# A two-layer hybrid trunk on one core: four small changes, and three branch outputs transposed by a detour through DRAM

## The chip, the cores and the metric

The kernel runs on one core of one Trainium2 chip. The metric is the device time of one execution in microseconds. A profile is one more execution, recorded by the hardware; its span is counted from the first to the last instruction of the core, and its own time lies a little above the span.

## The reference

Two layers with 256 tokens and a width of 2048. Cut to what matters:

```
for l in range(2):
    xn = rmsnorm(h, pre_norm_g[l])
    fq fk fv ff fg dq dk dv dg sz sxbc sdt su sg mg = columns of xn @ w_in[l]
    oa = forgetting_attention(fq, fk, fv, ff + b) * silu(fg)      # bias: cumsum(log_sigmoid(ff)), 4 heads
    ob = differential_attention(rope(dq), rope(dk), dv) * silu(dg)
    oc = mamba2_ssd(sz, sxbc, sdt)
    od = s5(su) * silu(sg)                                       # diagonal complex scan, gelu, GLU
    m  = sum_n sigmoid(mg[n]) * (o_n @ w_branch[l, n])           # each o_n has 512 columns, m has 2048
    h  = h + rmsnorm(m @ w_out[l], post_norm_g[l])
```

Inputs and output are float32.

## The kernel before, in words

**Tiles and staging.** Tokens lie in two blocks of 128 (`tb`). All weights of both layers are streamed once, as 298 chunks of 512 rows by 512 columns (524 for one segment), each four k-tiles of 128 rows. SyncE's queue loads a chunk into `raw` (1 MB, three buffers). float32 products are made from two rounded halves: ScalarE writes `wh`, the rounded weights, VectorE `wl`, the rest (`raw` − `wh`), both for two k-tiles at once (128x1024); the pools of `wh` and of `wl` hold five such pairs each. The input of a matmul is split in the same way into `xh` and `xl` (for a branch output `oh` and `ol`, for the merged sum `mh` and `ml`). For each k-tile and token block TensorE then does three matmuls of 128x512, `wh·xh` (L425), `wh·xl` (L426) and `wl·xh` (L427), into the accumulator `acc`. L115 is the helper `act` of ScalarE, L103, L109 and L112 are helpers of VectorE.

**Order.** `plan()` gives the column groups of a layer: first the thirteen input segments (fq fk fv bc fg dq dk dv dg xs sz su sg), then for the branches n = 0, 1, 2 (fox, diff, ssd) four pairs of a gate group `mg(n, cg)` of 16 k-tiles and a projection `br(n, cg)` of four, then the fourth branch (S5) with its GLU, then `out`, four groups. `group()` goes over the chunks of one group; a `hook` runs a function at one chunk of it.

**The branches.** Each is a generator, resumed between two chunks (`pump`) for a budget of work; `yield WAIT` makes it stop until the next chunk, and `drain` runs it to its end. The framework's scheduler then orders the instructions of each engine. In the fox generator, twelve float32 matmuls of 128x128 with broadcast operands (L480, L483) make the running sums of the log forget gates for the mask tiles `bm`. In S5, `prep_b` transposes `u`, splits it into `uu` and sends it to DRAM (`du`) and back (`s5u`); the drive matmul (L887) reads `s5u`, and a scan on VectorE (L905) follows.

**Branch outputs.** The output of a branch (`fxo`, `dfo`, `xst` for n = 0, 1, 2) has tokens on the partitions, and as input of `br(n, ...)` it must have channels there. `o_split`, hooked at chunk 2 of `mg(n, 0)`, does this with eight PE transposes (L300, by `split_T`), and ScalarE and VectorE split the result from PSUM into `oh` and `ol`. Elsewhere the kernel already transposes by a detour: `put` (L320) writes a tile to DRAM as four blocks of 32 columns by token, `get` (L326) reads it back as `shuf` with the blocks spread over partitions, both on GpSimd's queue, and VectorE's 32x32 transpose does the rest (`xT`, `foxqT`, `mT` and others).

**The ends.** At the start SyncE's queue brings the first columns of x and the first chunk in pieces; the gain `g0` comes on ScalarE's queue. At the end, for each token block, the square sum of the last output group is added up, a root is taken on VectorE, `y` is multiplied with the gain `pg` and added to `h` in four pieces of 512 columns, and SyncE sends each (L1210).

Of the kernel before, what the change touches and what calls it, by code (L numbers as in the profile page):

```python
# [23 lines left out]
PAD = 112  # L24
# [5 lines left out]
WAIT = -1  # L30
# [41 lines left out]
def trunk(ctx: ExitStack, tc: tile.TileContext, x, xT0, wall, cst, prm, rows, lam, normg, postg, s5b, s5c, out):  # L72
# [65 lines left out]
    g0 = cp.tile([128, KT], F32, name="g0")  # L138
    side = A.dma_start(out=g0, in_=prm[0, :, P_PRE:P_PRE + KT]).ins
    with tc.issue_after(side):  # L140
        act(warm, warm, AF.Exp)
    x0 = [wlp.tile([128, 4, 256], F32, tag="wl", name="x0") for _ in range(2)]
    load(x0[0], xT0[:, 0:4])
# [3 lines left out]
    strict_r = cp.tile([128, 128], F32R, name="strict_r")  # L147
    mask2 = cs[:, C_MK:C_MK + 256]
# [174 lines left out]
    def get(d):  # L323

        X = blk("shuf", (128, 4, 128))
        nc.gpsimd.dma_start(out=X, in_=d.rearrange("j (t i) c -> (j t) i c", i=4))  # L326
        return X
# [14 lines left out]
    def prefetch(spread=False, also=None):  # L342
# [6 lines left out]
        for k0, k1 in zip(cuts, cuts[1:]):  # L349
            load(raw[:, k0:k1], src[:, k0:k1])  # L350
# [113 lines left out]
    def fox(st):  # L464
# [316 lines left out]
    def s5(st):  # L781
# [55 lines left out]
        def prep_a(pc):  # L837
# [11 lines left out]
            uu, d = blk("uu", (128, 2, 256), F32R), dp.tile([128, 2, 256], F32R, tag="du", name="du")  # L849
            act(uu[:, 0], psu[:, 0:256])  # L850
            tt(uu[:, 1], psu[:, 0:256], uu[:, 0].bitcast(F32), SUB)
            ud[pc] = blk("ud", (128, 256))
            act(ud[pc], psu[:, 0:256], AF.Copy, scale=pk[:, l, P_D + pc:P_D + pc + 1])
# [82 lines left out]
        yield WAIT  # L936
        yield table(0)
# [28 lines left out]
    for l in range(L):  # L966
# [3 lines left out]
        if l == 0:  # L970
# [25 lines left out]
            def x_first(k):  # L996
                split_x(k, x0[k // 4][:, k % 4])

            prefetch(spread=True, also=x_first)
            load(x0[1], xT0[:, 4:8])  # L1000

# [12 lines left out]
            def more(c):  # L1014
# [6 lines left out]
                elif c == 7:  # L1021
                    prefetch()
                    load(cs, cst)
                    act(strict_r, strict)
                    load(pk, prm.rearrange("l p n -> p l n"))
# [43 lines left out]
        zz = small([128, 2, 12], "zz")  # L1069
# [32 lines left out]

        def turn_m(q):
            for tb in range(2):
                split_T(lambda i: mstat(tb, 4 * q, 4), m[tb][q], 4, scale=0.5)
        for gi, (kind, arg, ncol, nk) in enumerate(plan()):
            if kind == "in":
# [11 lines left out]
                group(xstat, nk, ncol, ev)  # L1119
                have.add(arg)  # L1120
            elif kind == "mg":
# [10 lines left out]
                def turn_o(n=n):  # L1132
                    if n < 3:
                        drain(("fox", "diff", "ssd")[n])
                    o_split(st, n)
                hook = {2: turn_o} if cg == (2 if n == 3 else 0) else None
# [52 lines left out]
            else:  # L1189
                cg = arg  # L1190
                if cg == 0:
                    yss = small([128, 2, 4], "yss")
# [135 lines left out]
```

## Time and profile before

| | |
|---|---|
| time, median of 3 runs | 1759.68 us (1759.61 to 1761.12) |
| time of the profiled execution | 1759.27 us |
| its span | 1757.4 us |
| TensorE busy | 1736.9 us (99%) |
| VectorE busy | 1340.6 us (76%) |
| ScalarE busy | 840.9 us (48%) |
| GpSimd busy | 87.4 us (5%) |
[...]
| moved by DMA | 356.51 MB, 203 GB/s in the mean |

Busy time is the time in which an engine has an instruction in work; waiting, and the issue of transfers, are not counted. TensorE's chain of waits, and not the shares of the others, says what an edit elsewhere is worth.

### The profile page before, as it was taken

How to read it: one execution, taken by the hardware profiler on the slowest of the kernel's cores; microseconds unless marked ns; L12 is line 12 of the kernel's file. 1: busy time of each engine (PE TensorE's matmuls, PEld its weight loads, DVE VectorE, ACT ScalarE, POOL GpSimd, SP SyncE). 2: the span in 40 equal slices, each digit the busy share in tenths (PEclk: the TensorE clock that was granted, in tenths of full speed). 3: DMA queues.
4: the chain of work that ended last, by engine and by line, in shares of the span. 5: the costliest groups of instructions: out<-in, count | busy, mean ns of one | idle time of the engine just before them, and what ended most of it. 6: DMA issues, size and time to landing. Idle time of an engine off the chain costs nothing.

```text
span 1757.4 us, 22117 instructions
## 1 busy us (share of the span) xinstructions
PE 1736.9 (99%) x8150; PEld 1438.2 (82%) x8150; DVE 1340.6 (76%) x2415; ACT 840.9 (48%) x1135; POOL 87.4 (5%) x146
## 2 busy tenths in 40 slices
PE   9999999999999999999999999999999999999997
PEld 7888888888888878888889888888888888788886
DVE  6765467997899999576674655669978999985854
ACT  7445445554444434444464444564544444444542
POOL 0000020000100000020000000100010000000100
PEclk9999999999999999999999999999999999999999
DMA  9664574455655655585555645744555655555752
GB/s 359 229 223 157 193 276 168 145 215 181 194 218 186 222 185 199 189 290 188 181 195 206 227 145 197 269 168 164 198 191 195 221 172 197 214 191 192 275 204 96
DMA packets 60813, 356.51 MB, mean 203 GB/s; under 512 B 7840, under 2 KB 12064, under 8 KB 22304
## 3 DMA queue, kind: packets, MB, share of 16 engines
q1 hardware_dynamic: 46640, 322.04, 51.2%
q0 software_dynamic: 13920, 33.04, 5.9%
q8 instruction: 64, 1.05, 0.2%
q14 instruction: 45, 0.37, 0.1%
q10 hardware_dynamic: 144, 0.01, 0.0%
HBM read 341.43 MB, written 13.63 MB: 202 GB/s over the span
## 4 chain that ended last, share of the span: by engine, by line
PE 85%; DVE 10%; issue 2%; DMA 2%; ACT 1%; SPq 0%; POOL 0%; DVEq 0%; ACTq 0%
PE acc L427 27%; PE acc L425 27%; PE acc L426 27%; DVE wl L103 3%; DVE Et L103 1%; DVE s5w L103 1%; DVE s5t L103 1%; PE mx L300 1%; DVE s5a L103 1%; DVE s5a L905 1%; PE mx L595 1%; DVE Etm L103 1%; PE mx L462 1%; DVE m L103 1%; DMA s5u<-du 1%
## 5 line engine op out<-in xcount | busy, mean ns | idle before, releaser
L115 ACT ACTIVATE wh<-raw 128x1024 fp32r<-128x1024 f32 (+1 forms) x586 | 619.0, 1061 | 730.9 <-PE acc L426 616.0
L103 DVE TENSOR_TENSOR wl<-raw,wh 128x1024 fp32r<-128x1024 f32 (+1 forms) x586 | 712.0, 1221 | 324.0 <-ACT wh L115 311.6
L425 PE MATMUL acc<-wh,xh 128*128 128x512 f32 (+1 forms) x1896 | 730.8, 386 | 1.2 <-ACT sig L115 1.2
L427 PE MATMUL acc<-wl,xh 128*128 128x512 f32 (+1 forms) x1896 | 725.6, 384 | 3.4 <-DVE wl L103 3.3
L426 PE MATMUL acc<-wh,xl 128*128 128x512 f32 (+1 forms) x1896 | 726.1, 383 | 0.0
L427 PEld LDWEIGHTS acc<-wl,xh 128*128 128x128 f32 x1896 | 355.4, 188 | 74.9 <-DVE wl L103 6.3
L425 PEld LDWEIGHTS acc<-wh,xh 128*128 128x128 f32 x1896 | 356.2, 188 | 71.6 <-ACT sig L115 2.1
L426 PEld LDWEIGHTS acc<-wh,xl 128*128 128x128 f32 x1896 | 356.3, 188 | 66.9
L425 PE MATMUL acc<-wh,oh 128*128 128x512 f32 x256 | 100.5, 393 | 0.0
L426 PE MATMUL acc<-wh,ol 128*128 128x512 f32 x256 | 99.8, 390 | 0.0
L427 PE MATMUL acc<-wl,oh 128*128 128x512 f32 x256 | 99.7, 389 | 0.0
L425 PE MATMUL acc<-wh,mh 128*128 128x512 f32 x224 | 87.5, 391 | 0.0
L427 PE MATMUL acc<-wl,mh 128*128 128x512 f32 x224 | 87.3, 390 | 0.0
L426 PE MATMUL acc<-wh,ml 128*128 128x512 f32 x224 | 87.2, 389 | 0.0
L115 ACT ACTIVATE sig<-acc,rhalf 128x512 f32<-128x512 f32 x64 | 42.7, 683 | 32.6 <-PE acc L427 24.9
L425 PEld LDWEIGHTS acc<-wh,oh 128*128 128x128 f32 x256 | 48.1, 188 | 10.5 <-issue 0.8
L427 PEld LDWEIGHTS acc<-wl,oh 128*128 128x128 f32 x256 | 48.1, 188 | 10.2
L426 PEld LDWEIGHTS acc<-wh,ol 128*128 128x128 f32 x256 | 48.1, 188 | 9.5
L427 PEld LDWEIGHTS acc<-wl,mh 128*128 128x128 f32 x224 | 42.1, 188 | 8.7
L426 PEld LDWEIGHTS acc<-wh,ml 128*128 128x128 f32 x224 | 42.1, 188 | 8.6
L425 PEld LDWEIGHTS acc<-wh,mh 128*128 128x128 f32 x224 | 42.1, 188 | 8.5
L905 DVE TENSOR_TENSOR_SCAN s5a<-S5R,s5w 128x256 f32<-128x256 f32 x64 | 40.4, 672 | 0.0
(339 smaller groups left out, 1376.6 us busy)
## 6 DMA issues: line engine op xcount, KB each, us to landing
raw<-in_wall_dram SPq DMA_DIRECT2D x290, 1024.0 KB, 4.8
shuf<-d POOLq DMA_DIRECT2D x36, 256.0 KB, 5.6
raw<-in_wall_dram SPq DMA_DIRECT2D x8, 1048.0 KB, 5.1
s5b<-in_s5b_dram POOLq DMA_DIRECT2D x16, 256.0 KB, 3.3
s5u<-du POOLq DMA_DIRECT2D x32, 128.0 KB, 3.6
d<-m POOLq DMA_DIRECT2D x12, 256.0 KB, 4.6
h<-in_x_dram SPq DMA_DIRECT2D x2, 1024.0 KB, 9.7
d<-ropea POOLq DMA_DIRECT2D x8, 256.0 KB, 2.8
```

The costliest lines, as they stand in the source:

```text
L103: V.tensor_tensor(out=out, in0=a, in1=b, op=op)
L115: A.activation(out, a, f, **kw)
L300: PE.transpose(ps[:, i * 128:(i + 1) * 128], src[:, i * 128:(i + 1) * 128], ident)
L425: PE.matmul(o, lhsT=sh, rhs=rh, start=k == 0, stop=False)
L426: PE.matmul(o, lhsT=sl, rhs=rh, start=False, stop=False)
L427: PE.matmul(o, lhsT=sh, rhs=rl, start=False, stop=k == nk - 1)
L462: PE.matmul(pso[:, c], lhsT=pt[:, b], rhs=v[b][:, c], start=b == 0, stop=b == nb - 1)
L595: PE.matmul(ps[:, a, 0:nk], lhsT=qT[hd // 2][a][:, hd % 2, qb * 128:(qb + 1) * 128], rhs=kT[hd // 2][:, hd % 2, 0:nk], start=True, stop=True)
L905: V.tensor_tensor_scan(out=a[:, r], data0=rr, data1=w[:, r], initial=0.0, op0=MUL, op1=ADD)
```

## The change

Five parts:

1. **Start.** The gain and the first k-tile of x are one tile `gx`, loaded by one transfer on ScalarE's queue; k-tile 1 and k-tiles 2 and 3 are loaded on SyncE's queue in turn with the pieces of the first chunk, and k-tiles 4 to 7 behind it.
2. **Bias.** Each of two key blocks is made by two matmuls of 128x512 in the rounded format (a product `fU` of the upper triangle and the gates, from VectorE, high and low half, against a column of ones). The second block takes its carry from the last column of `bm[hd][:, 1]`. The generator yields 2.2 and not 0.8.
3. **S5.** `ud` is made ahead of `uu`'s low half, and one more `yield WAIT` stands behind `prep_b(0)`.
4. **End.** In the last layer `y` is multiplied with the gain first, three of the four square sums are added ahead, `h` is updated in five pieces (512, 512, 512, 256, 256), and for the second token block every second piece is sent on ScalarE's queue.
5. **Branch outputs.** For n = 0, 1, 2 the eight PE transposes become `put` and `get` on ScalarE's queue, two of each per branch and layer, and one VectorE transpose of 128x512 per token block. The writes stand at chunk 0 of `sg`, of `mg(0, 3)` and of `mg(1, 3)`, each behind a `drain`; the reads at chunk 0 of `mg(n, 0)`; the transposes at chunk 2 of it, as before. The rows of `w_br` are permuted to fit.

```diff
-    def put(src):
+    def put(src, eng=nc.gpsimd):
         d = dp.tile([4, 128, 128], F32, tag="d", name="d")
-        nc.gpsimd.dma_start(out=d.rearrange("j n c -> n j c"), in_=src.rearrange("n (j c) -> n j c", j=4))
+        eng.dma_start(out=d.rearrange("j n c -> n j c"), in_=src.rearrange("n (j c) -> n j c", j=4))
...
         bm = [blk("bm", (128, 3, 128)) for _ in range(4)]
+        fh, fl = small([128, 2, 4], "fh", F32R, 1), small([128, 2, 4], "fl", F32R, 1)
+        V.tensor_copy(fh, lf[:, :, 0:4])
+        tt(fl, lf[:, :, 0:4], fh.bitcast(F32), SUB)
         for kb in range(2):
             ps = mx()
+            for j, a in enumerate((fh, fl)):
+                o = blk("fU", dt=F32R)
+                tt(o.rearrange("p (h t) -> p h t", h=4), U.unsqueeze(1).to_broadcast([128, 4, 128]),
+                   bc(a.bitcast(F32)[:, kb].unsqueeze(2), [128, 4, 128]), MUL)
+                PE.matmul(ps, lhsT=bc(one_r, [128, 128]), rhs=o, start=j == 0, stop=j == 1)
+            p3 = ps.rearrange("p (h k) -> p h k", h=4)
             for hd in range(4):
-                o = ps[:, hd * 128:(hd + 1) * 128]
-                PE.matmul(o, lhsT=bc(lf[:, 0, hd:hd + 1], [128, 128]), rhs=bc(one, [128, 128]) if kb else U,
-                          start=True, stop=kb == 0)
-                if kb:
-                    PE.matmul(o, lhsT=bc(lf[:, 1, hd:hd + 1], [128, 128]), rhs=U, start=False, stop=True)
-            p3 = ps.rearrange("p (h k) -> p h k", h=4)
-            for hd in range(4):
-                tt(bm[hd][:, 2 * kb], p3[:, hd], tri, ADD)
                 if kb == 0:
+                    tt(bm[hd][:, 0], p3[:, hd], tri, ADD)
                     act(bm[hd][:, 1], p3[:, hd])
-            yield 0.8
+                else:
+                    stt(bm[hd][:, 2], p3[:, hd], bm[hd][:, 1, 127:128], tri, ADD, ADD)
+            yield 2.2
...
+    def o_put(st, n):
+        for tb in range(2):
+            st["o", n, tb] = put(st["o", n, tb], A)
+
+    def o_get(st, n):
+        for tb in range(2):
+            st["o", n, tb] = get(st["o", n, tb], A)
     def o_split(st, n):
...
-            split_T(lambda i: (oh, ol), st["o", n, tb], 4)
+            if n == 3:
+                split_T(lambda i: (oh, ol), st["o", n, tb], 4)
+            else:
+                r = blk("oT", (128, 4, 128))
+                V.transpose(out=r.rearrange("p k (t i) -> p i k t", i=4),
+                            in_=st["o", n, tb].rearrange("p i (k c) -> p i k c", c=32))
+                act(oh, r)
+                tt(ol, r, oh.bitcast(F32), SUB)
...
         yield prep_b(0)
         yield WAIT
+        yield WAIT
         yield table(0)
...
+        def send_o(n):
+            drain(("fox", "diff", "ssd")[n])
+            o_put(st, n)
...
-                group(xstat, nk, ncol, ev)
+                group(xstat, nk, ncol, ev, hook={0: lambda: send_o(0)} if arg == "sg" else None)
...
-                hook = {2: turn_o} if cg == (2 if n == 3 else 0) else None
+                hook = {2: turn_o} if cg == (2 if n == 3 else 0) else {}
+                if n < 3 and cg == 0:
+                    hook[0] = lambda n=n: o_get(st, n)
+                if n < 2 and cg == 3:
+                    hook[0] = lambda n=n: send_o(n + 1)
...
+                    if l == L - 1:
+                        tt(yb[tb][3], last, pg[3], MUL)
+                        tt(s1, ysum[:, tb], yss[:, tb, 3:4], ADD)
+                        rsqrt(r1, s1, 1, 1.0 / D, EPS)
+                        rows = slice(tb * 128, (tb + 1) * 128)
+                        for i, (c0, c1) in enumerate(((0, 512), (512, 1024), (1024, 1536), (1536, 1792), (1792, 2048))):
+                            y = yb[tb][c0 // 512][:, c0 % 512:c0 % 512 + c1 - c0]
+                            stt(h[tb][:, c0:c1], y, r1, h[tb][:, c0:c1], MUL, ADD)
+                            (A if tb and i % 2 else nc.sync).dma_start(out=out[rows, c0:c1], in_=h[tb][:, c0:c1])
+                        return
```

TensorE, in the input segments of the first layer, where the mask tiles are made. Of before, the last matmul ahead of the bias and the bias (L480 and L483 are its two calls):

```order
L427 MATMUL acc<-wl,xh 128x512
L480 MATMUL mx<-cs,sp 128x128 x5
L483 MATMUL mx<-cs,sp 128x128
L480 MATMUL mx<-cs,sp 128x128
L483 MATMUL mx<-cs,sp 128x128
L480 MATMUL mx<-cs,sp 128x128
L483 MATMUL mx<-cs,sp 128x128
L480 MATMUL mx<-cs,sp 128x128
L483 MATMUL mx<-cs,sp 128x128
L425 MATMUL acc<-wh,xh 128x512
```

And of the change, the first of the two places, whose matmuls with weights have the lines L429 to L431 there; the second place comes a chunk later and has the same rows:

```order
L431 MATMUL acc<-wl,xh 128x512
L490 MATMUL mx<-fU,one_r 128x512 x2
L429 MATMUL acc<-wh,xh 128x512
L430 MATMUL acc<-wh,xl 128x512
L431 MATMUL acc<-wl,xh 128x512
```

Twelve matmuls in one place became two pairs in two places.

ScalarE, around the end of the diff branch in the first layer (`dfo` are its two outputs, `pt` its scores, `oh` the fox output). Before:

```order
L115 ACTIVATE pt<-mx 128x256
L115 ACTIVATE wh<-raw 128x1024 x2
L115 ACTIVATE pt<-mx 128x256
L115 ACTIVATE dfo<-mx 128x512
L115 ACTIVATE wh<-raw 128x1024 x4
L115 ACTIVATE oh<-mx 128x512 x2
L115 ACTIVATE wh<-raw 128x1024
```

And in the change, where L328 is a read and L322 a write on ScalarE's queue:

```order
L115 ACTIVATE pt<-mx 128x256
L328 DMA shuf<-d 128x512 x2
L115 ACTIVATE wh<-raw 128x1024 x2
L115 ACTIVATE pt<-mx 128x256
L115 ACTIVATE dfo<-mx 128x512
L322 DMA d<-dfo 128x4x128
L115 ACTIVATE wh<-raw 128x1024 x2
L115 ACTIVATE oh<-oT 128x512
L115 ACTIVATE wh<-raw 128x1024
L322 DMA d<-dfo 128x4x128
L115 ACTIVATE oh<-oT 128x512
```

The two writes of `dfo` stand between the splits of weights, the first right behind the copy of `dfo`'s second block; three `wh` and one `oh` stand between them.

VectorE, where the third branch's output is turned in the first layer. Before, `ol` is made from PSUM:

```order
L103 TENSOR_TENSOR wl<-raw,wh 128x1024
L103 TENSOR_TENSOR s5t<-s5a,Et 128x512
L103 TENSOR_TENSOR s5w<-s5a,Et 128x512
L103 TENSOR_TENSOR wl<-raw,wh 128x1024
L103 TENSOR_TENSOR ol<-mx,oh 128x512 x2
L103 TENSOR_TENSOR s5a<-s5w,s5t 128x256 x2
```

And in the change:

```order
L103 TENSOR_TENSOR wl<-raw,wh 128x1024
L103 TENSOR_TENSOR s5a<-s5w,s5t 128x256 x2
L103 TENSOR_TENSOR Et<-E_2976 128x256
L103 TENSOR_TENSOR Etm<-E_2977 128x256
L103 TENSOR_TENSOR Et<-E_2976,E_2977 128x256
L103 TENSOR_TENSOR Et<-Et,Etm 128x256
L103 TENSOR_TENSOR Etm<-E_2977,E_2976 128x256
L559 STREAM_TRANSPOSE oT<-shuf 128x4x128
L103 TENSOR_TENSOR Et<-Et,Etm 128x256
L103 TENSOR_TENSOR wl<-raw,wh 128x1024
L103 TENSOR_TENSOR ol<-oT,oh 128x512
L559 STREAM_TRANSPOSE oT<-shuf 128x4x128
```

The subtractions moved behind two transposes, which stand among the `wl` and the products of S5's table (`Et`, `Etm`); ScalarE's order has the two reads just behind the `wh` that belongs to the first `wl` shown.

## Rows read from the trace of the kernel before

**Rows 1.** The page, part 1: busy us, share of the span, instructions.

```profile
PE 1736.9 (99%) x8150; PEld 1438.2 (82%) x8150; DVE 1340.6 (76%) x2415; ACT 840.9 (48%) x1135; POOL 87.4 (5%) x146
```

**Rows 2.** Waits of TensorE: us in total, times, longest.

```profile
PE acc L427 <- DVE wl L103: 3.3, 6, 1.2
PE mx L887 <- DMA s5u<-du: 2.5, 2, 1.3
```

**Rows 3.** Timeline of TensorE, 327 to 331 us: start, us, operation.

```profile
327.56 0.39 PE L425 MATMUL acc<-wh,xh 128*128 128x512 f32 x1
...
328.93 1.03 PE L300 MATMUL mx<-cs,fxo 128*128 128x128 f32 x8
...
330.04 0.40 PE L426 MATMUL acc<-wh,xl 128*128 128x512 f32 x1
```

**Rows 4.** Timeline of TensorE, 493 to 626 us: in brackets the wait.

```profile
494.27 0.50 PE L427 MATMUL acc<-wl,xh 128*128 128x512 f32 x1 [0.23 <-DVE wl L103]
...
625.10 0.72 PE L427 MATMUL acc<-wl,xh 128*128 128x512 f32 x2 [1.19 <-DVE wl L103]
```

**Rows 5.** Timeline of TensorE, 144 to 149 us.

```profile
145.95 1.28 PE L480 MATMUL mx<-cs,sp 128*128 128x128 f32 x10
...
148.86 0.39 PE L426 MATMUL acc<-wh,xl 128*128 128x512 f32 x1
```

**Rows 6.** Timeline of the end.

```profile
1740.56 13.18 SPq L1210 DMA_DIRECT2D out_dram<-h  x8
...
1750.05 0.69 DVE L103 TENSOR_TENSOR y<-acc,pg 128x512 f32<-128x512 f32 x1
1750.65 2.73 DVE L112 SCALAR_TENSOR_TENSOR h<-y,yr,h 128x512 f32<-128x512 f32 x4
```

**Rows 7.** Groups of VectorE by form: count, busy us, mean ns, idle before.

```profile
L103 DVE TENSOR_TENSOR wl<-raw,wh 128x1024 fp32r<-128x1024 f32 x570 | 692.0, 1220 | 304.6 <-ACT wh L115 292.3 <-PE mx L300 5.8 <-PE mx L480 3.0
...
L103 DVE TENSOR_TENSOR Et<-Et,Etm 128x256 f32<-128x256 f32 x64 | 26.6, 416 | 0.0
...
L1097 DVE STREAM_TRANSPOSE mT<-shuf 128x512 f32<-128x512 f32 x12 | 12.3, 1080 | 0.0
```

**Rows 8.** Timeline of the start.

```profile
7.30 0.50 PE L425 MATMUL acc<-bwh,xh 128*128 128x512 f32 x1 [1.63 <-ACT bwh L115]
...
9.06 1.15 ACT L115 ACTIVATE bwh<-raw 128x512 fp32r<-128x512 f32 x2 [0.43 <-DMA raw<-in_wall_dram]
...
12.98 0.19 PEld L425 LDWEIGHTS acc<-wh,xh 128*128 128x128 f32 x1 [0.34 <-ACT wh L115]
```

**Rows 9.** The tile `shuf`: its reads (ns of issue), and their time to landing.

```profile
L326 POOL DMA_DIRECT2D shuf<-d x36: 537/554/563, 99.6 to 1644.4; - x36
...
DMA to landing us min/median/max: 2.9/5.6/9.8
```

**Rows 10.** Windows: stretch, length; busy us (count) PE, PEld, DVE, ACT, POOL; clock, DMA share, GB/s.

```profile
433.00:455.00 22.00, 20.68 (x96) 16.95 (x95) 16.87 (x27) 9.83 (x13) 4.10 (x7) 1.00 0.79 249
554.00:576.00 22.00, 22.00 (x105) 18.36 (x104) 22.00 (x40) 10.53 (x12) 0.00 (x0) 1.00 0.35 127
576.00:587.00 11.00, 11.00 (x61) 8.40 (x60) 8.04 (x10) 3.73 (x4) 0.00 (x0) 1.00 0.84 322
```

**Rows 11.** Timeline of ScalarE and VectorE, 317 to 332 us.

```profile
318.21 0.60 ACT L115 ACTIVATE dfo<-mx 128x512 f32<-128x512 f32 x1 [0.85 <-PE mx L462]
...
320.02 1.13 DVE L112 SCALAR_TENSOR_TENSOR dfo<-dfo,df_rst,dg 128x128 f32<-128x128 f32 x4
...
327.38 1.14 DVE L112 SCALAR_TENSOR_TENSOR dfo<-dfo,df_rst,dg 128x128 f32<-128x128 f32 x4
```

**Rows 12.** Waits of all engines: us in total, times, longest.

```profile
ACT wh L115 <- PE acc L426: 616.0, 405, 4.4
...
POOL d L320 <- DVE ropea L103: 254.5, 8, 119.3
```

More of the change, by code (lines that the diff above doesn't have):

```diff
@@ L23 @@
 KW = 576
-PAD = 112
+PAD = 120
 AHEAD = 1
@@ L136, in trunk @@
     V.memset(warm, 0.0)
-    g0 = cp.tile([128, KT], F32, name="g0")
-    side = A.dma_start(out=g0, in_=prm[0, :, P_PRE:P_PRE + KT]).ins
+    gx = blk("gx", (128, KT + 256))
+    side = A.dma_start(out=gx, in_=xT0[:, 0:KT + 256]).ins
+    g0, x0 = gx[:, 0:KT], [gx[:, KT:], blk("x0", (128, 256))]
+    xT0 = xT0[:, KT:].rearrange("p (k t) -> p k t", k=KT)
     with tc.issue_after(side):
         act(warm, warm, AF.Exp)
-    x0 = [wlp.tile([128, 4, 256], F32, tag="wl", name="x0") for _ in range(2)]
-    load(x0[0], xT0[:, 0:4])
+    x0 += [blk("x0", (128, 2, 256)), wlp.tile([128, 4, 256], F32, tag="wl", name="x0")]
     ident = cs[:, C_ID:C_ID + 128]
@@ L147, in trunk @@
     strict_r = cp.tile([128, 128], F32R, name="strict_r")
+    one_r = cp.tile([128, 1], F32R, name="one_r")
     mask2 = cs[:, C_MK:C_MK + 256]
@@ L314, in split_T, with get @@
             stt(dl, p3, scale, dh.bitcast(F32), MUL, SUB)
-    def put(src):
+    def put(src, eng=nc.gpsimd):
         d = dp.tile([4, 128, 128], F32, tag="d", name="d")
-        nc.gpsimd.dma_start(out=d.rearrange("j n c -> n j c"), in_=src.rearrange("n (j c) -> n j c", j=4))
+        eng.dma_start(out=d.rearrange("j n c -> n j c"), in_=src.rearrange("n (j c) -> n j c", j=4))
         return d
-    def get(d):
+    def get(d, eng=nc.gpsimd):
         X = blk("shuf", (128, 4, 128))
-        nc.gpsimd.dma_start(out=X, in_=d.rearrange("j (t i) c -> (j t) i c", i=4))
+        eng.dma_start(out=X, in_=d.rearrange("j (t i) c -> (j t) i c", i=4))
         return X
@@ L340, in trunk, with prefetch @@
     behind = [None]
-    def prefetch(spread=False, also=None):
+    def prefetch(spread=False, also=None, beside=None):
         ncol = chunks[woff[1]]
@@ L349, in prefetch @@
         for k0, k1 in zip(cuts, cuts[1:]):
+            if beside and k0:
+                beside(k0)
             load(raw[:, k0:k1], src[:, k0:k1])
@@ L996, in x_first @@
             def x_first(k):
-                split_x(k, x0[k // 4][:, k % 4])
-            prefetch(spread=True, also=x_first)
-            load(x0[1], xT0[:, 4:8])
+                split_x(k, x0[k] if k < 2 else x0[2][:, k - 2] if k < 4 else x0[3][:, k - 4])
+            prefetch(spread=True, also=x_first, beside=lambda k: load(x0[k], xT0[:, k] if k == 1 else xT0[:, 2:4]))
+            load(x0[3], xT0[:, 4:8])
             def more_x(c):
@@ L1024, in more @@
                     act(strict_r, strict)
+                    act(one_r, one)
                     load(pk, prm.rearrange("l p n -> p l n"))
@@ L1068, in trunk @@
         st["bc"] = [None, None]
-        zz = small([128, 2, 12], "zz")
+        zz = small([128, 2, 12], "zz", bufs=1)
         sp = small([128, 2, 12], "sp")
@@ L1191, in trunk @@
                 if cg == 0:
-                    yss = small([128, 2, 4], "yss")
+                    yss, ysum = small([128, 2, 4], "yss"), small([128, 2, 1], "ysum")
                     pg = [blk("pg") for _ in range(4)]
@@ L1208, in residual @@
                         stt(h[tb][:, c], yb[tb][q], r1, h[tb][:, c], MUL, ADD)
-                        if l == L - 1:
-                            nc.sync.dma_start(out=out[tb * 128:(tb + 1) * 128, c], in_=h[tb][:, c])
-                        else:
-                            split_T(lambda i: xnext(tb, 4 * q + i), h[tb][:, c], 4,
-                                    gcol=pk[:, l + 1, P_PRE + 4 * q:P_PRE + 4 * q + 4])
-                    if l < L - 1 and tb == 0:
+                        split_T(lambda i: xnext(tb, 4 * q + i), h[tb][:, c], 4,
+                                gcol=pk[:, l + 1, P_PRE + 4 * q:P_PRE + 4 * q + 4])
+                    if tb == 0:
                         prefetch()
@@ L1225, in ev @@
                         tt(yb[tb][cg], acc[0], pg[cg], MUL)
+                        if cg == 2 and l == L - 1:
+                            V.tensor_reduce(out=ysum[:, tb], in_=yss[:, tb, 0:3], axis=AX.X, op=ADD)
                 if cg == 3 and l < L - 1:
@@ L1257, in _layout @@
             elif kind == "br":
-                w = w_br[l, arg[0]][:, arg[1] * 512:(arg[1] + 1) * 512]
+                w = w_br[l, arg[0]][P if arg[0] < 3 else slice(None), arg[1] * 512:(arg[1] + 1) * 512]
             elif kind == "glu":
@@ L1306, in _layout @@
     s5b = s5b.reshape(L, 8, 2, 2, 128, 128).transpose(0, 1, 4, 2, 3, 5).reshape(L, 8, 128, 512)
-    xT0 = f("x").reshape(T, KT, 128).transpose(2, 1, 0)
+    xT0 = f("x").reshape(T, KT, 128).transpose(2, 1, 0).reshape(128, KT * T)
+    xT0 = np.concatenate([prm[0, :, P_PRE:P_PRE + KT], xT0], axis=1)
     return dict(x=f("x").reshape(T, D), xT0=xT0, wall=wall, cst=cst, prm=prm, rows=rows, lam=f("diff_lambda").reshape(L, 256),
```

6 lines of the change are left out of this document (2 added, 4 removed).

## The prediction

> **What bounds the kernel now.** I read the busy shares first [rows 1]. TensorE is busy for 1736.9 of the 1757.4 us of the span; VectorE works 76% of it. So the time is TensorE's instruction stream plus the few places where it stands. TensorE's list of waits gives those [rows 2]: after the start it waits for `wl` six times (3.3 us together) and for the tile `s5u` twice (2.5 us). A change can gain only by taking work out of TensorE's stream, by removing one of these waits, or at the two ends of the span, where TensorE does nothing. It can lose by making TensorE wait for a weight tile. Each pair of k-tiles needs `wh` from ScalarE and then `wl` from VectorE, so both engines have a deadline every 2.73 us: twelve matmuls at 0.228 us, which is the spacing of the six matmuls from 327.56 to 328.93 [rows 3].
>
> **The change, part by part**, against the profiled execution's own 1759.27 us; the median of the runs shown is 0.41 us higher.
>
> *Transposes.* Each layer loses eight 128x128 transposes per branch for three branches. The place of one group is seen on TensorE: the transposes begin at 328.93, and the second matmul behind them begins at 330.04, where one step of 0.23 would have been due had the first followed at once [rows 3]. So a group takes 1.11 − 0.23 = 0.88 us. Six groups give **−5.3 us** if TensorE has weights to go on with. Where VectorE is late anyway, the freed time becomes a longer wait for `wl`. TensorE's waits for it stand at 494 and 625 us of the first layer and at the same places of the second [rows 4], some 55 us behind the second and the third branch's transposes; only the first branch's, near 330, lie clear. So the bound is two groups, −1.8.
>
> *Bias.* The twelve small matmuls of a layer stand between 145.95 and the second matmul behind them at 148.86 [rows 5]: 2.91 − 0.23 = 2.68 us. In their place come four of 128x512; taken at the ordinary step they cost 4 × 0.23 = 0.92. That is 1.76 a layer, **−3.5 us** for two. If each held TensorE for the whole 0.39 of its row [rows 5], it would be −2.2, the other end. VectorE gets four 128x512 products of 0.69 each [rows 6], 2.8 us a layer; its eight additions of the mask stay. They lie beside the bias groups' matmuls, 350 us ahead of the first wait for `wl` [rows 4], so I cost them at nothing; uncovered, they would be 2.8 a layer.
>
> *S5.* The drive matmul comes one chunk later, so that `s5u` lands before TensorE asks for it. The two waits [rows 2] go: **−2.5 us**. A chunk is 4 × 2 × 3 = 24 matmuls, 5.5 us, more than twice the longer wait of 1.3. What is late next is the scan behind the drive, on VectorE, which has nothing to deliver to TensorE for many chunks. Bounds −2.5 and 0.
>
> *End.* Behind the last square-sum VectorE multiplies `y` with the gain (1750.05), then makes four updates in 2.73, and SyncE sends eight pieces, the last at 1740.56 + 13.18 = 1753.74 [rows 6]. The product moves ahead of the square root: −0.60, the step from 1750.05 to 1750.65. The last 512 columns are updated in two halves; at 0.68 a full and 0.42 a half update [rows 6, 7] the sum is 3 × 0.68 + 2 × 0.42 = 2.88, +0.15. The last transfer is half as large; from its issue at 1753.74 to the end of the span there are 3.66 us, of which I take back 0.5 (nothing to half, 1.8). Sum **−1.0**, ends −0.4 and −2.2.
>
> *Start.* The gain and the first two k-tiles arrive in one transfer, the next in small pieces. TensorE's first matmul at 7.30 waits for ScalarE, and could come sooner [rows 8]. But ScalarE's third weight piece, at 9.06, waits for a transfer with the same bytes ahead of it, and its chain from there still leads to TensorE's wait at 12.98. TensorE would only wait later. **0**, ends −1.6 (the whole wait before 7.30 gained) and +0.5.
>
> *VectorE's new work and its waits.* Per branch two transposes of 1.08 [rows 7] come onto VectorE, 2.2 us; its two subtractions stay. And a transpose stands in VectorE's queue until its read has landed. The existing reads of this shape, all on GpSimd's queue, need 2.9 to 9.8 us, 5.6 in the median [rows 9]. Between the issue of a read and the first transpose VectorE has, by the orders of the instructions, for the second branch one `wl` and five 128x256 products, 1.22 + 5 × 0.42 = 3.3 us; for the third two more of these, 1.22 + 7 × 0.42 = 4.2 [rows 7]. So it would wait 2.3 and 1.4 us. For the first branch there are two `wl` and some fifty short instructions, and no wait. The first branch's 2.2 us fall near 330, clear of the waits for `wl`, and cost nothing. The second's 2.2 + 2.3 = 4.5 come near 440 us, in a stretch of 22 us in which VectorE is idle for 5.1 [rows 10], and that takes them. The third's 2.2 + 1.4 = 3.6 come near 565: idle for nothing in 22 us, then for 3.0 in the next 11 [rows 10]. That leaves 0.6 a layer, 1.2 for two. Behind a late transpose stands the next `wl`, and TensorE waits for that. Where VectorE is behind, though, it reaches the transpose later than I count, and the read has landed by then. I take **+1.0** for both layers. The ends: −3.3, if the present waits for `wl` [rows 2] vanish, and +16, if of the 4.5 + 3.6 = 8.1 us a layer nothing is absorbed.
>
> [...]
>
> *ScalarE's queue.* It issues 24 transfers more, each perhaps as long as GpSimd's 0.55 [rows 9], 13 us over the span, beside 616 us in which it waits for a buffer [rows 12]. Worse are the writes that wait: the second branch's first write needs VectorE's last product, done at 321.15, and stands behind ScalarE's copy that is done at 318.81; the second write's products end at 328.52 [rows 11]. So ScalarE stands up to 2.3 us at the first, and at the second up to what is left of the 7.4 us between them after three `wh` of 1.15, 3.9. Behind the write stands the next `wh`, and TensorE waits for that. ScalarE's slack is large, though: its 405 waits for a buffer [rows 12] say that it is usually all five buffers ahead. With one pair in use four are ready, 4 × 2.73 = 10.9 us, less a `wh` (two halves of one took 1.15 [rows 8]) and a `wl` of 1.22, so 8.5 us. I cost the queue at nothing; the upper end is 12, the rival's below.
>
> The sum is −5.3 − 3.5 − 2.5 − 1.0 + 0 + 1.0 + 0 = −11.3, and 1759.27 − 11.3 = **1748.0 us**.
>
> **The rivals.**
>
> *VectorE keeps half of it.* If only half of the 8.1 us a layer is absorbed, the term is +8 instead of +1, and the time is 1755 (1752 to 1757). For it: what TensorE loses, 2.6 + 1.8 = 4.4 us a layer, brings each deadline for `wl` forward, the idle microseconds of now are then fewer, and the waits at 494 and 625 [rows 4] say that VectorE is short there already. Against it: each full stretch is followed by idle time, and a wait for a read overlaps with VectorE's arrears.
>
> *ScalarE is held by the writes.* [...] As a mechanism of this kernel: of the twelve writes, each would have to stand some 1 us beyond the slack of 8.5 to cost 12 us, which gives about 1759 (1756 to 1761). Against it: the two writes that I worked out [rows 11] stand 2.3 and 3.9 us.
>
> *Slower: the reads land late.* If every read takes the 9.8 us of the slowest row [rows 9] and nothing is absorbed, the second and third branch's first transposes wait 6.5 and 5.6 us, 12.1 a layer. Then VectorE's `wl` behind them are late by 24 us in two layers, and the time is 1748 − 1 + 24, about 1771. It decides from 11.3 / 2 = 5.7 us a layer on. For it: reads come in the stretches with the weights' own transfers, DMA share 0.79 near 440 [rows 10]. Against it: 9.8 is the extreme of 36, and VectorE's arrears hide part of a wait.
>
> *Still faster.* If the start gains its 1.6 and the waits for `wl` vanish, 1741 to 1745.
>
> **How the numbers follow.** The main case, 1745 to 1751, has 0.52; VectorE keeping half 0.20; ScalarE held 0.11; slower 0.09; still faster 0.08. 0.2%, 3.5 us, is about what a measurement of this kernel can tell from no change: from the median of 1759.68, faster is below 1756.2 and slower above 1763.2. Faster has the main case, the still faster one and most of VectorE's, 0.79; within it ScalarE's and the tail of VectorE's, 0.12; slower the late reads, 0.09. The range 1743 to 1758 holds the main case, VectorE's, half of the still faster one and a third of ScalarE's, 0.8 in all.
>
> **What would show it.** In the changed profile TensorE's busy time should be 8 to 9 us lower, with the bias's twelve records gone and of the transposes of branch outputs the fourth's left. Its list of waits should have no `s5u`, and some 3 to 5 us for `wl`; 10 or more would say that VectorE keeps the gain. The new transposes should show a wait of 1 to 3 us for `shuf` in the second and third branch; 5 or more would be the late reads. A wait of TensorE for `wh`, with a write before it in ScalarE's list, would be the held queue. The prediction is wrong if the waits behind 480 and 618 us grow by more than the 4.4 us that a layer gives.

## The result, and the profile after

The changed kernel takes 1744.88 us (median of 4 runs, 1744.48 to 1745.94) against 1760.22 us in the same comparison: a ratio of 0.9914, 95% interval 0.9901 to 0.9927, so 15.3 us faster. 1748.0 was forecast, with a range of 1743 to 1758: the sign and the range held, and the gain is 4 us larger than its forecast. The profiled execution took 1744.79 us, 14.5 less than before, with a span of 1743.0.

The page of the changed kernel, part 1, answers to [rows 1]:

```profile
PE 1726.2 (99%) x8062; PEld 1429.6 (82%) x8062; DVE 1355.9 (78%) x2443; ACT 842.9 (48%) x1136; POOL 87.4 (5%) x146
```

TensorE is busy for 10.7 us less (8 to 9 were forecast), VectorE for 15.3 more. TensorE's list of waits, against [rows 2]:

```profile
PE acc L429 <- ACT bwh L115: 2.5, 2, 1.4
PE acc L431 <- DVE wl L103: 2.3, 4, 1.1
```

The wait for `s5u` is gone, and the waits for `wl` did not grow, they fell from 3.3 us to 2.3. Two of them stand in each layer, in the first near 605 and 634 us; the one at 494 of [rows 4] is gone, and so is a wait for `sig` near 548 (0.46 and 0.78 us in the two layers of before):

```profile
605.28 0.50 PE L431 MATMUL acc<-wl,xh 128*128 128x512 f32 x1 [0.82 <-DVE wl L103]
...
633.54 0.50 PE L431 MATMUL acc<-wl,xh 128*128 128x512 f32 x1 [0.22 <-DVE wl L103]
```

Where the time went is read best from ScalarE's evacuations of `acc`: one that waits for the last matmul of its group starts when TensorE sets it free. The same evacuations in both timelines (us from the start of the span):

| evacuation, and what lies ahead of it | before | after | ahead by | step |
|---|---|---|---|---|
| `fk`: the start | 51.08 | 50.26 | 0.82 | 0.82 |
| `dv`: bias | 193.47 | 190.69 | 2.78 | 1.96 |
| `sig`: first branch's transposes | 334.78 | 331.07 | 3.71 | 0.93 |
| `sig`, 426: nothing changed | 426.14 | 422.67 | 3.47 | −0.24 |
| `sig`, 456: S5's drive, second branch | 456.34 | 450.38 | 5.96 | 2.49 |
| `sig`, 571: waits at 494 and 548, third branch | 571.13 | 562.78 | 8.35 | 2.39 |
| `junk`, 853: the rest of the layer | 852.78 | 844.58 | 8.20 | −0.15 |
| `fk` of layer 2: the change of layers | 922.91 | 915.69 | 7.22 | −0.98 |
| `dv` of layer 2: bias | 1065.32 | 1056.10 | 9.22 | 2.00 |
| `sig`, 1328: first and second branch, S5 | 1328.00 | 1315.84 | 12.16 | 2.94 |
| `sig`, 1443: third branch | 1443.16 | 1428.22 | 14.94 | 2.78 |
| last `junk` | 1747.22 | 1732.48 | 14.74 | −0.20 |
| end of the span | 1757.4 | 1743.0 | 14.4 | −0.34 |

Two of these rows in the timelines, at 456 and 571 before and the same two after:

```profile
456.34 0.69 ACT L115 ACTIVATE sig<-acc,rhalf 128x512 f32<-128x512 f32 x1 [1.20 <-PE acc L427]
...
571.13 0.69 ACT L115 ACTIVATE sig<-acc,rhalf 128x512 f32<-128x512 f32 x1 [1.21 <-PE acc L427]
```

```profile
450.38 0.69 ACT L115 ACTIVATE sig<-acc,rhalf 128x512 f32<-128x512 f32 x1 [1.15 <-PE acc L431]
...
562.78 0.69 ACT L115 ACTIVATE sig<-acc,rhalf 128x512 f32<-128x512 f32 x1 [1.14 <-PE acc L431]
```

Two larger losses: at the change of layers ScalarE waited 1.40 us for a chunk of `raw`, and TensorE behind it 1.05; and the end itself became 0.34 longer. Its timeline, against [rows 6]:

```profile
1732.48 0.60 ACT L115 ACTIVATE junk<-acc 128x512 f32<-128x512 f32 x1 [10.19 <-PE acc L431]
...
1733.20 0.69 DVE L103 TENSOR_TENSOR y<-acc,pg 128x512 f32<-128x512 f32 x1 [5.17 <-ACT junk L115]
1733.81 0.15 DVE L103 TENSOR_TENSOR ys<-ysum,yss 128x1 f32<-128x1 f32 x1
...
1735.84 0.16 DVE L168 SCALAR_TENSOR_TENSOR yr<-rq_t,rq_y 128x1 f32<-128x1 f32 x1
1736.04 2.87 DVE L112 SCALAR_TENSOR_TENSOR h<-y,yr,h 128x512 f32<-128x512 f32 x5
1736.82 2.45 SPq L1243 DMA_DIRECT2D out_dram<-h  x3
1737.48 1.40 ACTq L1243 DMA_DIRECT2D out_dram<-h  x2
```

The product `y` did move ahead of the root, but it stands on the same engine, waits for ScalarE's square of the same accumulator (`junk`), and the root's chain begins 0.61 us later for it.

The detour itself waits for nothing. The reads on ScalarE's queue land in 4.1 us in the median (page, part 6), and VectorE's transposes show no idle time ahead of them (its groups by form, last column):

```profile
shuf<-d ACTq DMA_DIRECT2D x12, 256.0 KB, 4.1
```

```profile
L559 DVE STREAM_TRANSPOSE oT<-shuf 128x512 f32<-128x512 f32 x12 | 13.0, 1086 | 0.0
```

In the second branch of the first layer the reads are issued 3.9 us ahead of the transpose:

```profile
434.32 0.82 ACTq L328 DMA_DIRECT2D shuf<-d  x2
...
438.22 1.08 DVE L559 STREAM_TRANSPOSE oT<-shuf 128x512 f32<-128x512 f32 x1
```

ScalarE does stand at a write, 2.76 us at the first one of the second branch (the timeline of ScalarE and its queue), and TensorE shows no wait behind it:

```profile
318.34 0.38 ACTq L322 DMA_DIRECT2D d<-dfo  x1
...
318.76 1.06 ACT L115 ACTIVATE wh<-raw 128x1024 fp32r<-128x1024 f32 x1 [2.76 <-DVE dfo L112]
```

### The profile page after: what moved, and what is told of

Its sections match the earlier page's. It is cut to its first block, busy times and chain, and to the rows that moved or that the text cites. A ratio compares the mean times of both kernels' runs of the same rounds, so it can differ in the third digit from the quotient of the medians.

```text
span 1743.0 us, 22005 instructions
## 1 busy us (share of the span) xinstructions
PE 1726.2 (99%) x8062; PEld 1429.6 (82%) x8062; DVE 1355.9 (78%) x2443; ACT 842.9 (48%) x1136; POOL 87.4 (5%) x146
## 4 chain that ended last, share of the span: by engine, by line
PE 86%; DVE 11%; issue 2%; DMA 1%; ACT 0%; DVEq 0%; ACTq 0%; SPq 0%
PE acc L429 27%; PE acc L431 27%; PE acc L430 27%; DVE wl L103 3%; DVE s5w L103 1%; DVE Et L103 1%; DVE s5t L103 1%; DVE s5a L103 1%; DVE s5a L930 1%; PE mx L620 1%; PE mx L466 1%; DVE m L103 1%; DVE mt L112 1%; DVE Etm L103 1%; PE mx L780 0%
## 5 line engine op out<-in xcount | busy, mean ns | idle before, releaser
L429 PE MATMUL acc<-wh,xh 128*128 128x512 f32 (+1 forms) x1896 | 731.2, 386 | 0.0
L431 PE MATMUL acc<-wl,xh 128*128 128x512 f32 (+1 forms) x1896 | 726.4, 384 | 2.3 <-DVE wl L103 2.3
L431 PEld LDWEIGHTS acc<-wl,xh 128*128 128x128 f32 x1896 | 355.8, 188 | 73.6 <-DVE wl L103 4.5
L429 PEld LDWEIGHTS acc<-wh,xh 128*128 128x128 f32 x1896 | 356.2, 188 | 71.6 <-ACT wh L115 2.1
L429 PE MATMUL acc<-wh,oh 128*128 128x512 f32 x256 | 100.1, 391 | 0.0
L431 PE MATMUL acc<-wl,oh 128*128 128x512 f32 x256 | 99.7, 389 | 0.0
L429 PE MATMUL acc<-wh,mh 128*128 128x512 f32 x224 | 87.5, 391 | 0.0
L431 PE MATMUL acc<-wl,mh 128*128 128x512 f32 x224 | 87.3, 390 | 0.0
L431 PEld LDWEIGHTS acc<-wl,oh 128*128 128x128 f32 x256 | 48.1, 188 | 10.3 <-DVE wl L103 0.2
L429 PEld LDWEIGHTS acc<-wh,oh 128*128 128x128 f32 x256 | 48.0, 188 | 9.6
L431 PEld LDWEIGHTS acc<-wl,mh 128*128 128x128 f32 x224 | 42.0, 188 | 8.7
L429 PEld LDWEIGHTS acc<-wh,mh 128*128 128x128 f32 x224 | 42.1, 188 | 8.6
```

Of the source, the lines that this page charges most:

```text
L429: PE.matmul(o, lhsT=sh, rhs=rh, start=k == 0, stop=False)
L431: PE.matmul(o, lhsT=sh, rhs=rl, start=False, stop=k == nk - 1)
```

## The experiments

Medians stand beside that of the kernel before on the same chip: 1759.87 for the first four, 1759.81 for the next four, 1759.53 for the last; the changed kernel's 1744.88 stands beside 1760.22. The kernels built from the one before with part 1, 2 or 5 also carry two small settings of the changed kernel, a padding tile of 120 columns instead of 112 and one buffer for `zz` instead of two; the start alone, which carries them too, shows no difference.

**Which part gains.** Each of the first four is the kernel before with some of the five parts, or all but one.

The detour, part 5, alone:

```diff
+            st["o", n, tb] = put(st["o", n, tb], A)
...
+            st["o", n, tb] = get(st["o", n, tb], A)
...
-            split_T(lambda i: (oh, ol), st["o", n, tb], 4)
```

> The kernel before with the detour of the three branch outputs alone. My theory, from the record: six groups of transposes go, 5.3 us, and VectorE gives 1.0 back: 1756, with the waits for s5u still there (2.5 us on TensorE's list). First rival: the detour itself also takes away the waits for wl near 494 us and for sig near 548 us, which are gone in the changed kernel (by TensorE's steps 1.0 and 1.7 us in two layers): 1752 to 1753. Second rival: VectorE keeps the gain and it was the other parts that made the changed kernel fast: 1758 or more.

Measured: 1760.65 us, ratio 1.0004 (0.9994 to 1.0013). No gain at all. TensorE's waits, and its timeline at the two of the first layer that grew or are new:

```profile
PE acc L427 <- DVE wl L103: 5.9, 6, 1.5
PE mx L904 <- DMA s5u<-du: 4.5, 2, 2.3
```

```profile
445.27 0.47 PE L904 MATMUL mx<-s5u,s5bs 128*128 128x256 f32 x2 [2.20 <-DMA s5u<-du]
...
572.42 0.50 PE L427 MATMUL acc<-wl,oh 128*128 128x512 f32 x1 [1.53 <-DVE wl L103]
```

The waits at 494 and 548 us are gone here too, as the first rival had it, but the time is lost elsewhere. The wait for `s5u` grew from 1.32 and 1.16 us to 2.20 and 2.31. The detour's two reads of 256 KB are issued at 437.5, and the four reads of `s5u` follow from 438.66 to 441.07; these land 5.7 to 6.0 us after their issue, where in the kernel before they need 4.6 to 5.2 (the tile `s5u` in this stretch). `uu`, from which they come, is made no later than before (435.12, and 435.42 before). Other kernels say the same: these four land in 4.6 to 5.0 us in the median of either layer where no such reads precede them (before, S5 alone, bias alone), in 5.0 to 5.9 behind the reads (changed, detour alone, the pair, changed without part 3), and in 4.0 and 4.2 where the reads stand behind them (the last experiment). So the reads delay `s5u`, and the drive waits for it. In the second layer the price is higher still, because behind the 2.31 us of standing TensorE's granted clock is lower for a while (windows of TensorE: stretch, length, busy, clock, DMA share, GB/s):

```profile
1314.40:1317.00 2.60, 0.28 (x3) 1.00 1.43 214
1317.00:1320.40 3.40, 3.40 (x10) 0.55 0.75 255
```

Seven matmuls there take 0.43 us from start to start instead of 0.23, another 1.4 us. The second loss is at 572: a new wait for `wl`. VectorE's timeline ahead of it:

```profile
564.38 1.22 DVE L103 TENSOR_TENSOR wl<-raw,wh 128x1024 fp32r<-128x1024 f32 x1
565.51 0.67 DVE L103 TENSOR_TENSOR ol<-oT,oh 128x512 fp32r<-128x512 f32 x1
566.10 1.07 DVE L551 STREAM_TRANSPOSE oT<-shuf 128x512 f32<-128x512 f32 x1
567.01 0.68 DVE L103 TENSOR_TENSOR s5t<-s5a,Et 128x512 f32<-128x512 f32 x1
...
571.13 1.24 DVE L103 TENSOR_TENSOR wl<-raw,wh 128x1024 fp32r<-128x1024 f32 x1
```

Between two `wl` stand 5.5 us of the third branch and of S5 together, twice the 2.73 us in which TensorE uses one up. Such a gap is not enough by itself: in the changed kernel 6.2 us stand between two `wl` (540.5 to 546.7), and TensorE does not wait. It then has more in hand. Counted by matmuls (a `wl` feeds four), the `wl` finished at 540.5 there is first used 6.6 us later, the one finished at 565.6 here 2.2 us later. From 557 to 569 us the changed kernel gets five `wl` in a row only 0.2 to 0.6 us before their use.

The opposite, parts 1 to 4 without the detour; against the changed kernel:

```diff
-            st["o", n, tb] = put(st["o", n, tb], A)
...
-            st["o", n, tb] = get(st["o", n, tb], A)
...
+            split_T(lambda i: (oh, ol), st["o", n, tb], 4)
```

> The changed kernel without the detour: start, bias, S5 and end. By the record -3.5 - 2.5 - 1.0 = -7.0, 1753. If the waits for wl near 494 and for sig near 548 go with the moved S5 drive and not with the detour: 1750. If the 1.0 us that the changed kernel loses at the change of layers belongs to one of these four, it shows here at 865 to 920 us.

Measured: 1755.43, ratio 0.9976 (0.9967 to 0.9985): 4.4 us faster, less than either number.

S5, part 3, alone (with `ud` ahead of `uu`'s low half):

```diff
         yield prep_b(0)
         yield WAIT
+        yield WAIT
```

> The kernel before with the S5 part alone (drive one chunk later, order of two evacuations). By the record -2.5; by TensorE's steps around the two waits, which are 1.57 and 1.41 longer than ordinary ones, -3.0: 1757.2. If the later drive also moves S5's work off the places near 494 and 548 us: -5.7, 1754.5. No gain would mean that VectorE's scan, later by a chunk, makes TensorE wait elsewhere.

Measured: 1760.32, ratio 1.0004 (0.9994 to 1.0013). The wait for `s5u` is gone, and TensorE's list has in its place:

```profile
PE acc L427 <- DVE wl L103: 4.5, 6, 0.9
...
PE mx L300 <- DVE s5t L103: 0.5, 2, 0.2
PE acc L426 <- DVE ol L103: 0.4, 2, 0.2
```

By the evacuations TensorE gains 1.6 us up to 456 and loses 3.1 from there to 571; a part of the 3.1 is only matmuls drawn ahead, and at 709 us this kernel is 0.1 behind the kernel before. The loss is not one of VectorE's load: this window takes 117.93 us here with VectorE busy for 110.50, and 112.40 with 110.03 in the changed kernel, where TensorE is busy all the time. (In the kernel before it takes 114.79 with 112.54; there 2.5 us more of VectorE's work fall into the window, so that pair alone would not tell load from order.) It is one of order: with the drive a chunk later S5's steps pile up between two `wl` (a wait of 0.76 at 517) and fall on the third branch's transposes, `ol` and the next `wl` (waits at 550, 569.6 and 570.8).

The end, part 4, alone:

```diff
+                    if l == L - 1:
+                        tt(yb[tb][3], last, pg[3], MUL)
+                        tt(s1, ysum[:, tb], yss[:, tb, 3:4], ADD)
```

> The kernel before with the end alone. By the record -1.0: 1759. By the changed kernel's own timeline, where the last square to the end of the span takes 10.52 us and not 10.18: +0.3, 1760.5, because the product stands ahead of the root on the same engine instead of behind it, and half the bytes land no sooner.

Measured: 1759.65, ratio 0.9997 (0.9988 to 1.0007): no difference that can be told.

**The pair.** Parts that gain nothing alone might gain together:

Here parts 3 and 5, and nothing else:

```diff
+            st["o", n, tb] = put(st["o", n, tb], A)
...
+            st["o", n, tb] = get(st["o", n, tb], A)
...
         yield prep_b(0)
         yield WAIT
+        yield WAIT
```

> The kernel before with the detour and the S5 part, nothing else. My theory now: neither gains alone, because without the later drive the wait for s5u takes up what the transposes free ahead of it, and without the detour the later drive bunches S5's work on VectorE near 545 to 572 us; together both hold: 1749.5 to 1751 (by the changed kernel's drift between 309 and 700 us of a layer, -5.4 and -5.5, so about -10.5 in all). If instead each part's own sum holds only with the bias or the start beside it, this stays at 1757 or more.

Measured: 1748.34, ratio 0.9939 (0.9924 to 0.9954), so 11.5 us faster by the medians, three quarters of the whole. Its waits for `wl` are those of the changed kernel (2.6 us, four times), and none for `s5u` is left. The two parts that are nothing each are worth 11 together.

And the changed kernel without part 3:

```diff
         yield prep_b(0)
         yield WAIT
-        yield WAIT
```

> The changed kernel without the S5 part. If S5's later drive is needed by the detour: as the detour alone (0) plus the bias (-4.0) plus the start (0 to -0.8): 1755 to 1756, with 4 to 5 us of waits for s5u. If the parts simply add: 1745 + 3 = 1748.

Measured: 1757.38, ratio 0.9991 (0.9981 to 1.0000). The waits of TensorE ahead of the first drive are back (1.7 us in the first layer, which the trace puts down to `Et`, and 3.0 in the second, to `s5u`), and so is the wait for `wl` at 569, 1.53 long in both layers, as in the detour alone. The parts do not add.

The start, part 1, alone:

```diff
+    gx = blk("gx", (128, KT + 256))
+    side = A.dma_start(out=gx, in_=xT0[:, 0:KT + 256]).ins
```

> The kernel before with the start alone. By the record 0. By the profiled executions the time of TensorE's first evacuation differs by up to 2.3 us among kernels with the same start, so the gain is a matter of the runs' spread: -0.8 to -1.5 in the median, and the spread, 3.4 us over 31 runs of the kernel before, falls to about 1.2 as in the two kernels that have the new start.

Measured: 1758.98 (1758.15 to 1762.29), ratio 0.9998 (0.9989 to 1.0007): no difference, and the spread did not fall either. The profiled executions show a source of the scatter: in seven of the fourteen kernels, with either start, 5 to 13 of TensorE's first matmuls take 0.43 us from start to start instead of 0.23, which costs 1.0 to 2.6 us. Without that the evacuation of `fk` stands at 50.6 to 51.1 us in the six kernels with the old start and at 50.0 to 50.7 in the eight with the new, so some 0.5 us may be the start's; the runs cannot tell it.

The bias, part 2, alone:

```diff
+                PE.matmul(ps, lhsT=bc(one_r, [128, 128]), rhs=o, start=j == 0, stop=j == 1)
```

> The kernel before with the bias alone. By the record -3.5; by the drift of the changed kernel between the third and the fifth attention segment -2.0 a layer, -4.0: 1756. But what is freed lies upstream of the wait for s5u: if that wait is bound to GpSimd's chain and not to TensorE, it grows by what is freed and the gain is smaller, down to 0. If it is bound to TensorE, as the moved evacuations are, the wait stays at 2.5 us.

Measured: 1755.98, ratio 0.9982 (0.9972 to 0.9992). The evacuations are 2.0 us a layer ahead, and the waits for `s5u` stay (1.41 and 1.36): what is freed ahead of that wait passes it, since `uu` comes earlier by as much. That settles how the detour alone loses there: not because TensorE comes sooner, but because `s5u` lands later.

**Is it the place of S5's steps, or only that `s5u` is there?** Two more kernels shift the drive further in the changed kernel.

```diff
         yield WAIT
         yield WAIT
+        yield WAIT
         yield table(0)
```

> The changed kernel with S5's drive one chunk later still. Theory of the phase: what matters is how VectorE's order interleaves S5's steps with the weight splits. In this order one stretch has some 9 us of other work between two wl at chunk 103 and three drives stand within one chunk near 110 to 111, against at most 6 us in the changed kernel: slower by 3 to 8 us, 1748 to 1753, with waits for wl near 590 to 640 us. Rival, that s5u only has to be there in time: a chunk more changes nothing, 1745.

Measured: 1771.31, ratio 1.0066 (1.0049 to 1.0083), slower than the kernel before and 26 us slower than the changed one; the direction was expected, the size is three times the largest expected. TensorE's waits:

```profile
PE acc L431 <- DVE wl L103: 9.4, 8, 2.5
PE acc L429 <- DVE mt L112: 5.0, 2, 2.5
PE mx L912 <- DVE s5y L103: 2.8, 2, 1.4
```

Up to 506 us it is level with the changed kernel, and at 678 it is 13.05 us behind, and another 14.1 by the end. VectorE's timeline shows the place: ten microseconds between two `wl`, filled with S5's steps and evacuations:

```profile
590.68 1.23 DVE L103 TENSOR_TENSOR wl<-raw,wh 128x1024 fp32r<-128x1024 f32 x1 [2.29 <-ACT wh L115]
...
594.63 1.26 DVE L112 SCALAR_TENSOR_TENSOR mt<-sig,acc 128x512 f32<-128x512 f32 x2
...
602.10 1.21 DVE L103 TENSOR_TENSOR wl<-raw,wh 128x1024 fp32r<-128x1024 f32 x1
```

It is idle for 2.29 us just ahead of that pile. What TensorE waits for there is not a `wl`: it has no such wait between 566 and 630 us, and the split of weights that ScalarE begins at 599.80 waited 6.43 us for TensorE, which so long had to use up what it had. It waits for the accumulator that `mt` frees (2.49 at 595.44) and for a tile `mx` in PSUM that `s5y` frees (1.32 at 605.53), and both stand in VectorE's queue behind S5's steps. The long waits for `wl` follow at 630 and 640. So the pile is where the forecast had it, but what came late first was another delivery of VectorE. Nor is the whole price VectorE's: behind some of these waits TensorE's granted clock falls (windows as above, for TensorE alone: stretch, length, busy, clock, DMA share, GB/s):

```profile
590.00:600.00 10.00, 7.51 (x29) 0.83 0.30 107
...
640.00:650.00 10.00, 9.75 (x36) 0.83 0.54 210
```

In the two layers together 33 matmuls take 0.43 us from start to start instead of 0.23, 6.6 us in all.

```diff
         yield WAIT
         yield WAIT
+        yield WAIT
+        yield WAIT
         yield table(0)
```

> The changed kernel with S5's drive two chunks later. Theory of the phase: in this order the drives are spread again and no more than 6.5 us of other work stands between two wl: as the changed kernel within 2 us, 1743 to 1747, although the chunk in between is slower. Rival, that the drive should be as early as its data allows: slower than with one more chunk.

Measured: 1746.88, ratio 0.9930 (0.9915 to 0.9945), 2 us behind the changed kernel and 24 ahead of the one between. `s5u` is in time in all three kernels, so being in time is not all that decides; the rival is refuted, and the drive need not be early either.

From the evacuation `sig` at 426 us to one at 720 us (`gt`; both times as in the kernel before), where most of the first layer's branches lie, four kernels with the detour give VectorE nearly the same work and need very different times for it:

| kernel | stretch | VectorE busy |
|---|---|---|
| changed | 289.56 us | 274.60 us |
| detour alone | 294.86 us | 274.75 us |
| drive one chunk later still | 302.49 us | 275.86 us |
| drive two chunks later | 290.47 us | 275.00 us |

**The end without the product on VectorE.**

```diff
-                        tt(yb[tb][3], last, pg[3], MUL)
+                        ya = blk("ya")
+                        act(ya, last)
+                        nc.gpsimd.tensor_tensor(out=yb[tb][3], in0=ya, in1=pg[3], op=MUL)
```

> The changed kernel with the last layer's last product taken from VectorE: ScalarE copies the accumulator to SBUF behind its square, and GpSimd multiplies it with the gain while VectorE takes the root. My theory: the product stands on VectorE's chain in both kernels, before the root instead of behind it, for 0.61 us; without it the end is 0.6 shorter: 1744.3. It is no gain if GpSimd's product takes longer than the root and three updates, some 4 us.

Measured: 1746.35, ratio 0.9926 (0.9911 to 0.9941): no gain. The timeline of the end:

```profile
1734.74 1.26 POOL L1238 TENSOR_TENSOR y<-ya,pg 128x512 f32<-128x512 f32 x1 [9.59 <-ACT ya L115]
1734.78 1.24 DVE L112 SCALAR_TENSOR_TENSOR rq_t<-rq_y,rq_v 128x1 f32<-128x1 f32 x1
```

The product left VectorE's chain, but an operation of one element in each partition, 0.22 us elsewhere, ended only with GpSimd's product. From the last square to the end of the span it is 10.92 us, against 10.52.

**The detour on GpSimd's queue.**

```diff
-            st["o", n, tb] = put(st["o", n, tb], A)
+            st["o", n, tb] = put(st["o", n, tb])
...
-            st["o", n, tb] = get(st["o", n, tb], A)
+            st["o", n, tb] = get(st["o", n, tb])
```

> The changed kernel with the detour's writes and reads on GpSimd's queue instead of ScalarE's. If the writes hold ScalarE at a cost (my third rival): 1 to 4 us faster, 1741 to 1744. If ScalarE has the slack that I worked out: no gain there, and on GpSimd's queue the writes stand ahead of S5's transfers and wait for the branch's last product, so 1745 or up to 5 us slower.

Measured: 1750.32, ratio 0.9954 (0.9939 to 0.9968), 5.4 us slower than on ScalarE's queue. There the reads stand behind S5's transfers (issued at 439.74 and not at 434.32), and VectorE waits for them, as it nowhere does on ScalarE's queue (its groups by form, and TensorE's waits):

```profile
L559 DVE STREAM_TRANSPOSE oT<-shuf 128x512 f32<-128x512 f32 x12 | 13.0, 1085 | 7.1 <-DMA shuf<-d 7.1
```

```profile
PE acc L431 <- DVE wl L103: 6.9, 8, 1.7
```

This is the forecast's rival of late reads in small: two waits for a late read, 7.1 us in all, cost some 5.

## Why the prediction was right, and where its sum was off

The total of 1744.88 lies just below the main case (1745 to 1751), in the band of the still faster one, but not for that rival's reasons: the start gained nothing that can be told, and the waits for `wl` did not vanish. The sum added up parts as if each stood alone; four of the five show no gain alone. That it came out near is in part luck: the terms were off in both directions.

**Transposes, −5.3.** Right in TensorE's stream: 0.84 in the first branch (0.93 with 0.09 of a smaller step ahead of it) against 0.88. But it is not theirs alone: the detour alone is worth nothing.

**Bias, −3.5.** −2.0 a layer, −4.0 in all by TensorE's steps, and 3.2 us (1.4 to 4.9) by the ratio with the part alone. Two of the new matmuls take 0.47 us, as worked out (145.16 to 145.63). The 2.0 are 0.2 more than the 1.76 that were worked out, and the kernels with the bias lose about as much again in the next stretch (the table's −0.24 at 426); why stays open. VectorE's products cost nothing: TensorE has no wait there.

**S5, −2.5.** The step that failed as it was put: "what is late next is the scan behind the drive, on VectorE, which has nothing to deliver to TensorE for many chunks". The scan and the steps behind it stand in VectorE's queue ahead of `wl` (in S5 alone from 510.97 on, ahead of the `wl` at 516.02, for which TensorE waits 0.76 us), and alone the part gives back between 456 and 709 us all that it gained. Beside the detour the two places give 1.57 and 1.41 by TensorE's steps, 3.0 and not 2.5, since a wait costs TensorE more than its label (below).

**VectorE, +1.0.** Sign and size wrong. The reads were waited for nowhere, where 2.3 and 1.4 us were worked out: in the second branch they are issued at 434.32, VectorE reaches the transpose at 438.22, 3.9 us later and not 3.3, and the read has landed by then, sooner than the 5.6 taken. The waits for `wl` fell by 1.0 us and those for `sig` by 1.2 by their labels, some 3 us by TensorE's steps. I had −3.3 as an end and argued from amounts, idle microseconds in windows against added ones. The experiments show that the order counts: with 275 to 276 us of VectorE's work the stretch of the table above takes 289.6, 290.5, 294.9 or 302.5 us.

**End, −1.0, and start, 0.** The end is +0.34 in the timeline and nothing in the medians: the step "the product moves ahead of the square root: −0.60" fails since the product still stands on the same chain, and half the bytes landed no sooner (4.0 us from the end of the last update to the end of the span before, 4.1 after). The accumulator was read by one engine after the other: `y`, which does not read `junk`, starts at 1733.20, when ScalarE's work on the accumulator ends (1733.16), and in the first token block at 1722.32, behind 1722.30. The start's 0.82 is within what the runs scatter.

**ScalarE's queue, 0.** Right: it stands 2.76 us where 2.3 was worked out, and TensorE has no wait for a `wh` behind it. Taking the detour off ScalarE's queue gained nothing either, though that run also made the reads late and so cannot tell the two apart. ScalarE's waits for a buffer, the slack, fell from 616 us to 573.

The sum by parts comes to −11.3; what it missed is mainly the pair, −11.5 by the medians (−10.5 by its profiled execution) where the sum had −6.8. The change of layers took back 1.0, by a `raw` chunk that landed late. All kernels here that have parts 1, 2, 4 and 5 together show it, with S5's part or without; those that have only some of them do not. What decides it stays open.

## What to carry to other kernels

Before adding up parts, ask whether they share a queue: two changes that were nothing alone were worth 11 us together, and one of them shifted by one more chunk cost 26. On an engine that is nearly full, read what stands ahead of each delivery to the bound engine (weights, which it uses up in 2.73 us each, but also the accumulators that it needs back) and how much that engine then has in hand, not the idle time in a window. An operation moved "off the chain" must also leave the chain's engine, and must not hold that engine up from where it goes, as GpSimd's product did (1.24 us instead of 0.22).

## What the runs showed of the hardware

- A wait costs TensorE more than its label: 0.23 us for `wl` at 494.27 in [rows 4] stretched two steps from 0.45 to 0.96 us (493.65 to 494.61), 0.50 in all; one of 0.46 at 548.33 cost 0.71.

```profile
493.65 0.39 PE L425 MATMUL acc<-wh,xh 128*128 128x512 f32 x1
...
494.61 0.40 PE L426 MATMUL acc<-wh,xl 128*128 128x512 f32 x1
```

- A wait of 2.31 us in the detour alone left TensorE with a granted clock of 0.55 in the next 3.4 us, where the mean of that execution is 0.997, and matmuls of 0.43 us from start to start; one of 2.20 in the other layer did not (1.00 from 444 to 452 us). Behind the start of the kernels, such stretches of 6 to 13 matmuls follow five more waits of TensorE in the profiled executions: 2.49, 2.42, 2.48 and 2.47 us with the drive one chunk later still, and 3.03 without part 3.
- A VectorE operation of one element in each partition (`rq_t`) took 1.24 us instead of 0.22 beside the GpSimd product of the end without the product on VectorE; the two end together, at 1736.02 and 1736.00 us.
- In the detour alone, transfers of 128 KB issued 1.2 us behind two of 256 KB on another engine's queue took about 1 us longer to land than before, 5.7 to 6.0 us instead of 4.6 to 5.2.
